# A sixth Strassen group, early branch weights, early bias sums and tanh gates in an encoder layer on one core

## The chip, the cores and the metric

The kernel runs on one core of a Trainium2 chip. Its engines are TensorE (PE in the profile; its weight loads are PEld), VectorE (DVE), ScalarE (ACT), GpSimd (POOL) and SyncE (SP), which here only issues DMA transfers. The metric is device time in microseconds (us). The kernel before took 1932.01 us (median of three runs, 1930.99 to 1932.27).

## What is computed

One encoder layer on 1024 tokens of width 1024, all in fp32:

```python
h = x + 0.5 * swiglu(rms_norm(x, n1), wg1, wu1, wd1)      # FFN 1, hidden width 2816
u = rms_norm(h, nm)
z = u @ w_in                                              # 1024 x 4352: qA kA vA qB kB vB gA gB
yA = neighbourhood_attention_2d(qA, kA, vA, rpb)          # 8 heads of 64, learned bias, band mask
yB = windowed_gqa_sink(rope(qB), rope(kB), vB, sink)      # 8 query heads, 2 key heads, window 128
merged = sigmoid(gA) * (yA @ w_branch_a) + sigmoid(gB) * (yB @ w_branch_b)
h = h + merged @ w_out
h = h + 0.5 * swiglu(rms_norm(h, n2), wg2, wu2, wd2)      # FFN 2
return rms_norm(h, nf)
```

## The kernel before

Every large fp32 product is made of three products of numbers with shortened mantissa: each operand is split into a high part (a cast on ACT, line 93) and a low part (a subtraction, line 94, on DVE or on POOL), and `mm3` (lines 142 to 150) multiplies high by high, high by low and low by high. So each block costs matmuls on PE, one cast on ACT and one "lo split" on DVE or POOL.

The stages follow one another in time as they do in the reference. FFN 1's gate and up products (0 to about 430 us) and most of the input projection (640 to 840 us) are made by Strassen's method in `products`: a group of two pairs of column blocks takes seven smaller products for each half, 14 products of 12 matmuls, 128 x 512 each. The input projection has 34 column blocks: five groups (20 blocks) go through `products`, and 14 gate blocks are left. These are made by `gate` as plain products of 48 matmuls each, and serve as filler between the small steps of attention. The down products of the FFNs and the product with `w_out` are Strassen products too, in the class `Down`: a list of entries (77 for FFN 1: seven products P2, P1, P5, P6, P3, P7, P4 by 11 blocks), each of which is prepared by `prep` (operands summed on DVE or POOL, two hi and two lo splits) up to seven entries ahead of PE and then multiplied in 12 matmuls. `loads` holds further calls by entry; `evict` (line 602) adds finished sums to the result.

Attention (840 to 1122 us) runs over 64 units, 32 of windowed attention and 32 of neighbourhood attention, in a pipeline of three: `scores` of one unit, `turn` (transposes, softmax's values split) of the one before, `values` of the one before that, and `filling` between them, which draws steps of six matmuls from `filler`: the gate blocks, then branch B (`branch_b`, the eight column blocks of yB @ w_branch_b times its gate), then the first two blocks of branch A. For each of the eight heads of neighbourhood attention `load_bias` (line 1089) adds the bias to two masks on DVE, in the middle of attention. What `filler` has left at the end of attention is drained at once; the rest of branch A and the preparation of the product with `w_out` come next.

The program text is written in the order of the work, and a scheduler then gives each engine its own list of instructions, in which each engine works strictly in order; a few are pinned to their place. SP and POOL issue DMA transfers, also in order. Buffers come from rings by tag: `raw` (four), `ws` (eight), `xs` (two), `hs` (six), and PSUM banks by tags `g` and `d`, four each.

Of the kernel before, what the change touches and what calls it, by code (L numbers as in the profile page):

```python
# [36 lines left out]
def trunk_kernel(ctx, tc, x, xt, n1, wg1, wu1, wd1, nm, win, rpb, sink, wa, wb, wo,  # L37
# [54 lines left out]
    def split(dst_hi, dst_lo, src, eng=None):  # L92
        nc.scalar.copy(dst_hi, src)  # L93
        (eng or nc.vector).tensor_tensor(dst_lo, src, f32v(dst_hi), op=ALU.subtract)  # L94
# [139 lines left out]
    def products(src, n, after, at_end, extra, ring, by_hand=False, last=PRODUCTS):  # L234
# [34 lines left out]
        def load_ahead(i):  # L269

            for m in range(2):
                ahead[i, m] = main.tile([P, 1024], F32, tag="ws", bufs=8, name=nm_("ahead"))
                fetch(ahead[i, m], i, m, 0)
# [14 lines left out]
        def pieces(q):  # L288

            i, p, m = seq[q]  # L290
            if i and (i, p, m) in early:
                a = ahead[i, m][:, 512 if p == "P2" else 0:][:, :512]
# [95 lines left out]
    def behind(prods):  # L388

        run, load_ahead = prods[2:4]  # L390

        def post(t):
            if t >= 3:
                drain(run, 10)
            if t in (3, 4):
                load_ahead(t - 2)

        return post
# [278 lines left out]

    def behind_ffn1(n):
        down.at_end(n)
        if n <= 60 and spread:  # L680
            nc.sync.dma_start(*spread.pop(0))

# [194 lines left out]
    groups = [[(12, 13), (14, 15)], [(16, 17), (0, 1)], [(4, 5), (8, 9)], [(2, 3), (6, 7)], [(10, 11), (18, 19)]]  # L877
# [62 lines left out]

    pin = tc.keep_in_program_order
# [65 lines left out]

    def keep_u():

        h, l = rhs(T4)  # L1010
        for i in range(2):
            r = raw4()
            nc.sync.dma_start(r.rearrange("p (t f) -> p t f", t=2), u_d[2 * i:2 * i + 2].rearrange("t p f -> p t f"))
            cols = slice(i * 256, i * 256 + 256)
            v = [a[:, :, cols].rearrange("p c (t x) -> p c t x", t=2) for a in (h, l)]
            split(v[0], v[1], r.rearrange("p (t c x) -> p c t x", t=2, c=4))
# [41 lines left out]
    hook(2, gate_first)  # L1058
    hook(1, keep_u)
    pg = products(lambda i, m, half: w_cols(win[0], groups[i][m][half] * P), NG, store_z, at_end, (2, 3), range(8, 16),  # L1060
                  last=("P1", "P2", "P5", "P6", "P7", "P4", "P3"))
    down.into(transition(down1, gain, to_strassen, behind(pg), 2), pg)
# [4 lines left out]
    mask_a = masks[:, :768].rearrange("p (s k) -> p s k", s=2)  # L1067
    mask_b = masks[:, 768:]
    nc.sync.dma_start(mask_a, c_mask_a.rearrange("s p k -> p s k"))
# [12 lines left out]
    def bias_slot(s):  # L1082
        return fa[:, 768 * s:768 * s + 768].rearrange("p (e k) -> p e k", e=2)

    def load_bias(s, h):
        braw = raw4()[:, :384]
        nc.sync.dma_start(braw, bias_d[h])
        for e in range(2):
            nc.vector.tensor_tensor(bias_slot(s)[:, e, :].rearrange("p (d r w) -> p d r w", d=3, r=ROWS),
                                    braw.rearrange("p (r d w) -> p d r w", d=3, w=8),  # L1090
                                    mask_a[:, e, :].rearrange("p (d r w) -> p d r w", d=3, r=ROWS), op=ALU.add)

    def prep_a(hp):
# [18 lines left out]
        yield  # L1112
        yield
        yield
# [31 lines left out]
    def fetch_branch(r, w, dc):  # L1146
        nc.sync.dma_start(r.rearrange("p (c f) -> p c f", f=P), w_cols(w, dc * P))
        return r

    def branch_w(w, dc, eng=None, r=None):  # L1150

        t = ws4()
        if r is None:
            r = fetch_branch(raw4()[:, :512], w, dc)
        split(t[:, :512], t[:, 512:], r, eng)
        return [t[:, k:k + 512].rearrange("p (c f) -> p c f", f=P) for k in (0, 512)]

# [13 lines left out]
    def split_y(slots, r0, eng):  # L1171
# [6 lines left out]
        split(h, l, r, eng)  # L1178

    a_order = [dc for p in range(4) for dc in (p, p + 4)]  # L1180
    a_mm, a_raw = [], {}
# [391 lines left out]
```

## Time and profile before

| | us |
|---|---|
| median of three runs | 1932.01 |
| profiled execution | 1931.21 |
| its span | 1929.4 |
| PE busy | 1919.3 |
| DVE busy | 1434.0 |
| ACT busy | 944.2 |
| POOL busy | 296.1 |

The granted clock was 0.999 in this execution. A row of the timeline has the start, the duration, the engine, the line, the operation, and "output<-inputs" by the program's names with the tile sizes; in square brackets stands the idle time before it and what ended it. A row of the waits has engine, line and tile, what it waited for, the total, the number of times and the longest. A row of a table of windows has the window, then its length, then PE, PEld, DVE, ACT and POOL busy (number of instructions), the granted clock, the share of the DMA engines and GB/s. A matmul's duration is pipelined: the next one starts before it ends. PE is busy in 99% of the span.

### The profile page before, as it was taken

To read this page: it belongs to the slowest core of one execution; us is meant where nothing else is said; L and a number is where in the kernel's file an instruction comes from. 1 tells how busy PE (TensorE), PEld (TensorE's weight loads), DVE (VectorE), ACT (ScalarE), POOL (GpSimd) and SP (SyncE) were. 2 spreads that over 40 slices of the span, in tenths; PEclk is the share of its full clock that TensorE was granted. 3 is DMA by queue.
4 is the path that set the end of the run, shared out by engine and by line. 5 is a ranking of instruction groups with operands and counts; after the bars stand their busy time and mean duration, and the time that the engine had idled before them with its cause. 6 is when DMAs were issued, how large, how long until landed. Compare 5 with 4: busy or idle time off the path is not lost.

```text
span 1929.4 us, 25478 instructions
## 1 busy us (share of the span) xinstructions
PE 1919.3 (99%) x8956; PEld 1602.7 (83%) x8956; DVE 1434.0 (74%) x2560; ACT 944.2 (49%) x1826; POOL 296.1 (15%) x432
## 2 busy tenths in 40 slices
PE   9999999999999999999999999999999999999998
PEld 8888888888888888888888888888888888888886
DVE  8987765668957778678888856889676566569864
ACT  7532333344446543477777862365333333344453
POOL 0011100013300112211122231010111001005210
PEclk9999999999999999999999999999999999999999
DMA  6244323285334467753459676443422322493341
GB/s 267 95 167 166 138 100 125 87 298 215 92 106 138 158 202 240 218 166 102 116 130 195 188 240 212 170 153 121 147 98 103 127 87 106 145 340 114 115 142 61
DMA packets 151745, 298.70 MB, mean 155 GB/s; under 512 B 14912, under 2 KB 64448, under 8 KB 151616
## 3 DMA queue, kind: packets, MB, share of 16 engines
q1 hardware_dynamic: 123072, 210.53, 33.3%
q0 software_dynamic: 27824, 85.48, 13.3%
q8 instruction: 71, 1.16, 0.2%
q10 hardware_dynamic: 720, 1.05, 0.1%
q14 instruction: 58, 0.48, 0.1%
HBM read 210.50 MB, written 88.27 MB: 155 GB/s over the span
## 4 chain that ended last, share of the span: by engine, by line
PE 96%; DVE 2%; ACT 1%; DMA 0%; issue 0%; POOLq 0%; POOL 0%; DVEq 0%
PE g L145 18%; PE g L147 18%; PE g L149 18%; PE d L149 12%; PE d L145 12%; PE d L147 12%; PE d L1315 2%; PE g L1329 1%; PE d L1294 1%; PE d L1295 1%; PE g L1334 1%; PE d L138 1%; DVE ar L94 0%; DMA ahead<-in_w_in_dram 0%; DMA n1c<-in_ffn_norm_dram 0%
## 5 line engine op out<-in xcount | busy, mean ns | idle before, releaser
L145 PE MATMUL g<-ar,ws 128*128 128x512 f32 x1128 | 422.6, 395 | 0.3 <-DVE fa L602 0.3
L147 PE MATMUL g<-ar,ws 128*128 128x512 f32 x1128 | 416.7, 390 | 0.0
L149 PE MATMUL g<-ar,ws 128*128 128x512 f32 x1128 | 416.3, 390 | 0.0
L145 PE MATMUL d<-ar,ws 128*128 128x512 f32 x736 | 281.9, 390 | 0.5 <-ACT ws L309 0.5
L147 PE MATMUL d<-ar,ws 128*128 128x512 f32 x736 | 281.4, 389 | 0.1
L149 PE MATMUL d<-ar,ws 128*128 128x512 f32 x736 | 281.2, 389 | 0.1
L149 PEld LDWEIGHTS g<-ar,ws 128*128 128x128 f32 x1128 | 211.7, 188 | 44.8
L147 PEld LDWEIGHTS g<-ar,ws 128*128 128x128 f32 x1128 | 211.8, 188 | 44.6
L145 PEld LDWEIGHTS g<-ar,ws 128*128 128x128 f32 x1128 | 206.4, 188 | 36.4 <-issue 0.7
L312 DVE TENSOR_TENSOR ws<-raw,ws 128x512 fp32r<-128x512 f32 x204 | 139.3, 689 | 98.9 <-ACT ws L309 97.9
L309 ACT CAST ws<-raw 128x512 fp32r<-128x512 f32 x204 | 125.0, 620 | 142.2 <-PE g L149 63.8
L145 PEld LDWEIGHTS d<-ar,ws 128*128 128x128 f32 x736 | 138.1, 188 | 29.4 <-ACT ws L309 0.9
L147 PEld LDWEIGHTS d<-ar,ws 128*128 128x128 f32 x736 | 138.1, 188 | 29.3 <-DVE ar L814 0.5
L149 PEld LDWEIGHTS d<-ar,ws 128*128 128x128 f32 x736 | 138.1, 188 | 29.1 <-DVE ws L312 0.5
L93 ACT CAST ws<-raw 128x512 fp32r<-128x512 f32 (+1 forms) x121 | 81.0, 669 | 144.7 <-PE d L149 66.7
L94 DVE TENSOR_TENSOR ws<-raw,ws 128x512 fp32r<-128x512 f32 (+1 forms) x119 | 94.0, 792 | 60.7 <-ACT ws L93 60.5
L415 POOL DMA_DIRECT2D hid<-fx x91 | 49.3, 542 | 432.3 <-DVE fx L475 288.6
L93 ACT CAST ar<-raw 128x512 fp32r<-128x512 f32 (+1 forms) x83 | 56.0, 679 | 93.7 <-PE g L147 55.0
L94 DVE TENSOR_TENSOR ws<-ar,ws 128x512 fp32r<-128x512 f32 x114 | 98.2, 866 | 4.0 <-ACT ws L93 3.9
L145 PE MATMUL g<-ws,ws 128*128 128x512 f32 x232 | 90.9, 392 | 0.0
L149 PE MATMUL g<-ws,ws 128*128 128x512 f32 x232 | 90.4, 390 | 0.0
L147 PE MATMUL g<-ws,ws 128*128 128x512 f32 x232 | 90.3, 389 | 0.0
(313 smaller groups left out, 3604.8 us busy)
## 6 DMA issues: line engine op xcount, KB each, us to landing
raw<-hid SPq DMA_DIRECT2D x70, 512.0 KB
hid<-fx POOLq DMA_DIRECT2D x91, 256.0 KB, 2.3
ar<-in_ffn_w_down_dram SPq DMA_DIRECT2D x32, 512.0 KB
raw<-in_ffn_w_up_dram SPq DMA_DIRECT2D x31, 512.0 KB
raw<-in_ffn_w_gate_dram SPq DMA_DIRECT2D x27, 512.0 KB
raw<-in_w_in_dram SPq DMA_DIRECT2D x27, 512.0 KB
hid<-fa POOLq DMA_DIRECT2D x51, 256.0 KB, 2.6
ar<-zs_d POOLq DMA_DIRECT2D x48, 256.0 KB, 5.0
```

The costliest lines, as they stand in the source:

```text
L93: nc.scalar.copy(dst_hi, src)
L94: (eng or nc.vector).tensor_tensor(dst_lo, src, f32v(dst_hi), op=ALU.subtract)
L138: nc.tensor.transpose(pt[:, c * P:(c + 1) * P], xs[:, (half * 4 + c) * P:(half * 4 + c + 1) * P], ident)
L145: nc.tensor.matmul(b, lhs[0], r[0], start=first, stop=False, **kw)
L147: nc.tensor.matmul(b, lhs[0], r[1], start=False, stop=False, **kw)
L149: nc.tensor.matmul(b, lhs[1], r[0], start=False, stop=last, **kw)
L309: nc.scalar.copy(w[0][:, :512], a)
L312: nc.vector.tensor_tensor(w[0][:, 512:], a, f32v(w[0][:, :512]), op=ALU.subtract)
L415: nc.gpsimd.dma_start(hid[PRODUCTS.index(p), i], src)
L1294: nc.tensor.matmul(b[:, :nw], un["q"][s], un["kd"][s][:, k0 * P:k1 * P], start=True, stop=False)
L1295: nc.tensor.matmul(b[:, :nw], un["q"][s], un["kl"][s][:, k0 * P:k1 * P], start=False, stop=True)
L1315: nc.tensor.transpose(pt[:, i * P:(i + 1) * P], un["pr"][s][:, i * P:(i + 1) * P], ident)
```

## The change

Five things are changed together.

- The blocks 20 to 23 (four gate blocks) become a sixth Strassen group of the input projection, so `gates` has 10 entries instead of 14. The ring of its operand tiles, the early loads of the first two groups (`early_rooms`, `sooner`) and the fetch of `u` (`fetch_u`) are adapted.
- The 16 blocks of the branch weights are split on ACT and DVE behind FFN 1's products (`wab_fetch`, `wab_split`, `wab_put`), one block in every four products, and kept in DRAM (`wab_d`) in split form. In the branches `fetch_w` loads them on POOL's queue.
- The sums of bias and mask (two for each of eight heads) are made behind the entries of the first down product (`bias_fetch`, `bias_add`, `bias_put`: a fetch at entry 2 + 6h, the adds at 5 + 6h, the write at 10 + 6h) and kept in DRAM (`bm_d`). In attention `fetch_bias` loads them.
- The gates use tanh: sigmoid(g) = (1 + tanh(g/2))/2, with (tanh + 1) times the product in one instruction and the factor 1/2 put into the product with `w_out` (0.5 for 1.0).
- The y splits move from POOL to DVE, filling follows a new table of shares (`n_b` = 46 units at 40/46 twice, then 0.8, then 1.5), and the value sums of two heads are made by one instruction where there were two.

The core of the diff:

```diff
-    groups = [[(12, 13), (14, 15)], [(16, 17), (0, 1)], [(4, 5), (8, 9)], [(2, 3), (6, 7)], [(10, 11), (18, 19)]]
+    groups = [[(12, 13), (14, 15)], [(16, 17), (0, 1)], [(4, 5), (8, 9)], [(2, 3), (6, 7)], [(10, 11), (18, 19)],
+              [(20, 21), (22, 23)]]
...
+    def bias_add(h):
+        for e in range(2):
+            o = biased[0][4 + e]
+            pin(nc.vector.tensor_tensor(o.rearrange("p (d r w) -> p d r w", d=3, r=ROWS),
+                                        biased[0][2 + h % 2].rearrange("p (r d w) -> p d r w", d=3, w=8),
+                                        biased[0][e].rearrange("p (d r w) -> p d r w", d=3, r=ROWS), op=ALU.add))
...
+    for h in range(8):
+        for e, f in ((2, bias_fetch), (5, bias_add), (10, bias_put)):
+            k = e + 6 * h
+            down.loads.setdefault(k, []).insert(0, lambda d, f=f, h=h: f(h))
...
+    def wab_split(i):
+        r, h, l = cast[i], hs(F32R), hs(F32R)
+        pin(nc.scalar.copy(h, r))
+        pin(nc.vector.tensor_tensor(l, r, f32v(h), op=ALU.subtract))
+        cast[i] = h, l
+
+    def wab_put(i):
+        for k, a in enumerate(cast.pop(i)):
+            nc.gpsimd.dma_start(wab_d[i, :, k * 512:k * 512 + 512], a)
...
     def behind_ffn1(n):
         down.at_end(n)
         if n <= 60 and spread:
             nc.sync.dma_start(*spread.pop(0))
+        for e, f in ((4, wab_put), (2, wab_split), (0, wab_fetch)):
+            i, k = divmod(80 - e - n, 4)
+            if k == 0 and 0 <= i < 2 * NC8:
+                f(i)
...
+    def fetch_w(i):
+        t = ws4()
+        nc.gpsimd.dma_start(t, wab_d[i])
+        mix["w", i] = [t[:, k:k + 512].rearrange("p (c f) -> p c f", f=P) for k in (0, 512)]
+
+    def open_gate(dc):
+        r = mix["rb", dc]
+        pin(nc.scalar.activation(r, r, AF.Tanh, scale=0.5))
...
             for n in range(2):
                 sl = slice(n * 512, (n + 1) * 512)
-                nc.vector.tensor_tensor(merged(dc)[:, sl], bs[n], rb[:, sl], op=ALU.mult)
+                nc.vector.scalar_tensor_tensor(out=merged(dc)[:, sl], in0=rb[:, sl], scalar=1.0, in1=bs[n],
+                                               op0=ALU.add, op1=ALU.mult)
...
-    rate = (nfill - 44) / 64.0
-    spent = 3.0
-
-    def filling(share):
+    n_b = 46
+    spent = 0.0
+
+    def filling(n):
         nonlocal spent
-        spent += rate * share
+        spent += len(gates) * 4 / n_b if n < n_b else 0.8 if n < 60 else 1.5
         drain(fill, int(spent))
         spent -= int(spent)
...
-    down = Down(4, wo[0], 1.0, place, quarter, {k: left_d[i] for i, k in enumerate(("P5", "P6", "P3", "P7"))},
+    down = Down(4, wo[0], 0.5, place, quarter, {k: left_d[i] for i, k in enumerate(("P5", "P6", "P3", "P7"))},
```

How the lists of the engines change is seen at two places. The lines of the new code are some ten further on: the split is line 98 (94 before), the sums of `prep` are L572 and L574 (L561 and L563 before), and L705 is the add of bias and mask. DVE in the first down product, kernel before; `raw` holds the hidden values, `ar` the weights, and each pair of L94 rows is the lo splits of one entry:

```order
529 L561 TENSOR_TENSOR ar_3100<-ar_3479,ar_3100 128x512
530 L94 TENSOR_TENSOR ws_3623<-raw_3501,ws_3623 128x512
531 L94 TENSOR_TENSOR ws_3624<-ar_3100,ws_3624 128x512
532 L561 TENSOR_TENSOR ar_3100<-ar_3479,ar_3100 128x512
533 L94 TENSOR_TENSOR ws_3644<-raw_3549,ws_3644 128x512
534 L94 TENSOR_TENSOR ws_3645<-ar_3095,ws_3645 128x512
535 L563 TENSOR_TENSOR ar_3095<-ar_3100,ar_3095 128x512
```

The same entries in the changed kernel, where the two adds of one head stand ahead of the splits of entry 23:

```order
552 L572 TENSOR_TENSOR ar_3230<-ar_3621,ar_3230 128x512
553 L98 TENSOR_TENSOR ws_3793<-raw_3695,ws_3793 128x512
554 L98 TENSOR_TENSOR ws_3794<-ar_3225,ws_3794 128x512
555 L705 TENSOR_TENSOR hs_3495<-hs_3493,hs_3491 128x384
556 L705 TENSOR_TENSOR hs_3496<-hs_3493,hs_3492 128x384
557 L574 TENSOR_TENSOR ar_3225<-ar_3230,ar_3225 128x512
558 L98 TENSOR_TENSOR ws_3814<-raw_3695,ws_3814 128x512
559 L98 TENSOR_TENSOR ws_3815<-ar_3225,ws_3815 128x512
```

Such a pair stands in this list eight times, six entries apart, and nothing else moved between these rows.

DVE at the end of branch B, kernel before. `ar_10187` is the product of gate and branch, `ar_10554` and `ar_10679` hold `w_out`, and the last value product has long been written:

```order
1654 L1213 TENSOR_TENSOR ar_10187<-g_10448,xs_10443 128x512
1655 L1213 TENSOR_TENSOR ar_10187<-g_10449,xs_10443 128x512
1656 L94 TENSOR_TENSOR ar_10717<-ar_10554,ar_10717 128x512 x2
1657 L561 TENSOR_TENSOR ar_10554<-ar_10679,ar_10554 128x512
1658 L1437 TENSOR_TENSOR raw_10540<-g_10481,raw_10540 128x512
1659 L1437 TENSOR_TENSOR raw_10540<-g_10482,raw_10540 128x512
```

The changed kernel at the same place. `g_10554`, `g_10601` and `g_10620` are the value products of the last three units, L1348 and L1351 write them to `fa`, and `ar_10642` and `ar_10757` hold `w_out`:

```order
1664 L1281 SCALAR_TENSOR_TENSOR ar_9531<-xs_10381,g_10450 128x512
1665 L1348 TENSOR_TENSOR s_771_6976<-g_10554,s_771_6976 64x256
1666 L1351 TENSOR_TENSOR fa<-g_10554,s_771_6976 64x128 x2
1667 L98 TENSOR_TENSOR ws_10571<-d_10573,ws_10571 128x2x128
1668 L98 TENSOR_TENSOR ws_10572<-d_10578,ws_10572 128x2x128
1669 L98 TENSOR_TENSOR ar_10792<-ar_10642,ar_10792 128x512
1670 L1348 TENSOR_TENSOR s_771_6976<-g_10601,s_771_6976 64x256
1671 L572 TENSOR_TENSOR ar_10642<-ar_10757,ar_10642 128x512
1672 L1351 TENSOR_TENSOR fa<-g_10601,s_771_6976 64x128 x2
1673 L575 TENSOR_TENSOR ar_10757<-ar_10757 128x512
1674 L1348 TENSOR_TENSOR s_771_6976<-g_10620,s_771_6976 64x256
```

The split of a `w_out` block (row 1669) now stands ahead of the writes of the last two units. On SP the eight loads of `w_out` go out as three of `ar_10757`, two of `ar_10642`, a gate block, two of `ar_10642` (the first of these is the one that row 1669 needs) and one of `ar_10757`; before, that block was the fifth.

More of the change, by code (lines that the diff above doesn't have):

```diff
@@ L1260, in units_a @@
             qs, kd, kl, va = heads_a[hp]
-            for s in range(2):
-                load_bias(s, 2 * hp + s)
             for j in range(NTT):
@@ L1379, in trunk_kernel @@
     drain(fill)
-    t = new_ar(2, F32)
-    for i in range(2, NC8):
-        a_raw[i] = fetch_branch(t[:, (i - 2) // 2, i % 2 * 512:i % 2 * 512 + 512], wa[0], a_order[i])
-    split(slot(22), slot(23), fa[:, 3072:4096])
+    for i in range(4, 6):
+        fetch_w(NC8 + i)
     for t in range(4):
```

218 lines of the change are left out of this document (129 added, 89 removed).

## The prediction

> **What bounds the kernel now.** I read the engine table of the page first, then the waits of PE, then its timeline.
>
> ```profile
> PE 1919.3 (99%) x8956; PEld 1602.7 (83%) x8956; DVE 1434.0 (74%) x2560; ACT 944.2 (49%) x1826; POOL 296.1 (15%) x432
> PE g L733 <- POOL ident masks.py:199: 1.5, 1, 1.5
> PE d L145 <- ACT ws L309: 0.5, 1, 0.5
> PE d L1315 <- DVE ws L94: 0.3, 1, 0.3
> PE g L145 <- DVE fa L602: 0.3, 1, 0.3
> 99.62 0.39 PE L147 MATMUL g<-ar,ws 128*128 128x512 f32 x1
> ...
> 100.98 0.39 PE L147 MATMUL g<-ar,ws 128*128 128x512 f32 x1
> 994.47 0.71 PE g L1329 x6
> ```
>
> PE waits 2.6 us in the whole span, so TensorE issue is the bound nearly everywhere and a matmul taken out should show in full. Its price is the step between starts, not the 0.39 us shown: six steps from 99.62 to 100.98 are 1.36 us, 0.227 us each. The 256-column value matmuls take 0.71/6 = 0.12 us. Every other engine matters only where it becomes late. So the question is where the moved work stands beside an engine that is already full, and the windows answer that (columns: PE, PEld, DVE, ACT, POOL busy):
>
> ```profile
> 300.00:420.00 120.00, 120.00 (x531) 99.41 (x530) 71.41 (x109) 44.91 (x78) 11.40 (x21) 1.00 0.42 148
> 460.00:520.00 60.00, 60.00 (x266) 49.70 (x265) 59.59 (x66) 25.54 (x45) 29.68 (x18) 1.00 0.27 84
> 700.00:800.00 100.00, 100.00 (x443) 82.81 (x442) 80.84 (x116) 39.13 (x67) 22.13 (x41) 1.00 0.76 235
> 1020.00:1080.00 60.00, 60.00 (x364) 53.13 (x363) 52.69 (x163) 49.05 (x125) 10.36 (x19) 1.00 0.76 171
> 1180.00:1240.00 60.00, 60.00 (x267) 49.67 (x266) 57.97 (x89) 21.43 (x35) 8.70 (x16) 1.00 0.57 202
> ```
>
> DVE is full in two places: the first down product (59.59 of 60) and the start of the wo product (57.97 of 60). In FFN 1 it has 49 us free of 120, in the input projection 19 of 100, in attention 7 of 60.
>
> **The Strassen group (L939 to L943 of the new code).** Four plain gate blocks of 48 matmuls go, 192; one group of 14 products of 12 comes, 168. That is 24 matmuls of 512 columns fewer, 24 x 0.227 = **-5.4 us**. The group's side work runs where DVE uses 80.84 of 100, and 14 products are 38 us with about 31 us of DVE work beside them; cost nothing, covered by those 19 us in 100. It also takes 44 us of filler from attention, which branch B and the first of branch A now fill.
>
> **Branch weights behind FFN 1.** Sixteen casts on ACT and sixteen lo splits on DVE, of the shape of these rows:
>
> ```profile
> L312 DVE TENSOR_TENSOR ws<-raw,ws 128x512 fp32r<-128x512 f32 x204 | 139.3, 689 | 98.9 <-ACT ws L309 97.9
> L309 ACT CAST ws<-raw 128x512 fp32r<-128x512 f32 x204 | 125.0, 620 | 142.2 <-PE g L149 63.8
> ```
>
> That is 0.62 and 0.69 us, one pair in each 10.9 us of PE (four products). FFN 1 has DVE free for 4.4 us in each such stretch. Taken as nothing; its cover would be gone only if DVE were past 94% there. The 32 writes on POOL's queue stand behind `hid` writes that nothing waits for soon, the 16 loads on SP ahead of weights that are fetched eight products early. Both ends: 0 and one missed pair, 0.7 us.
>
> **Bias and mask sums behind the down product.** Eight pairs of adds leave attention and enter the first down product.
>
> ```profile
> L1089 DVE TENSOR_TENSOR fa<-raw,masks 128x384 f32<-128x384 f32 x16 | 8.5, 549 | 0.1
> 936.90 1.02 DVE L1089 TENSOR_TENSOR fa<-raw,masks 128x384 f32<-128x384 f32 x2
> 482.85 0.69 DVE L563 TENSOR_TENSOR ar<-ar,ar 128x512 f32<-128x512 f32 x1
> 483.45 0.68 DVE L94 TENSOR_TENSOR ws<-raw,ws 128x512 fp32r<-128x512 f32 x1
> 484.06 1.78 DVE L94 TENSOR_TENSOR ws<-ar,ws 128x512 fp32r<-128x512 f32 x1
> 485.88 0.69 DVE L563 TENSOR_TENSOR ar<-ar,ar 128x512 f32<-128x512 f32 x1
> 483.68 1.61 POOL L566 TENSOR_TENSOR ar<-ar,ar 128x512 f32<-128x512 f32 x1 [1.42 <-DVE ar L563]
> 516.47 1.78 DVE L94 TENSOR_TENSOR ar<-ar,ar 128x512 fp32r<-128x512 f32 x1
> 518.17 0.68 DVE L94 TENSOR_TENSOR ar<-raw,ar 128x512 fp32r<-128x512 f32 x1
> 519.64 0.39 PE L145 MATMUL g<-ar 128*128 128x512 f32 x1
> ```
>
> In the full stretch one entry costs DVE 485.88 - 482.85 = 3.03 us, while PE needs 12 x 0.227 = 2.72, so the lead of the splits shrinks by 0.3 us an entry. The smallest lead is at entry 33: its lo split ends at 516.47 + 1.78 = 518.25, PE starts on it at 519.64, a lead of 1.4 us. After that POOL is out of the way and the lead grows again. The new order puts the pairs before entries 11, 17, 23, 29, 35 and so on; those before 17, 23 and 29 lie in the full stretch. A pair is 1.02 us of busy time and, back to back, about 0.94 us of DVE (an add is 0.47 from start to start: the pair of 1.02 less one 0.55), so three are 2.8 us. Less the 1.4 us of lead: **+1.4 us** of PE standing. Ends: 0, if DVE's slow splits absorb the adds, and 4.7 us, if each pair costs one more stretched split as at 484.06 (three times 1.78 - 0.68 = 1.1 on top). I take 1.4: in the order each pair stands between a lo split and L574 (L563 before), the instruction that releases POOL, so POOL is idle while they run. Their loads and writes on SP (a fetch three entries before the add, the write five behind it) wait for adds that DVE has already passed; what is queued there is the next weights, with five entries of slack. DVE gains the 8.5 us in attention.
>
> The stretched split beside POOL's L566 (1.78 against 0.68 us; it ends 0.55 us after POOL does) is what the Trainium skill, "SBUF — State Buffer", section "Who interferes with whom", describes: a DVE instruction with two inputs in SBUF contends with a GpSimd instruction that reads SBUF, and the one that issues first keeps the shared pair for its whole length. The trace agrees; by that rule an add that met L566 would pay up to 1.61 us, which is the third case below.
>
> **Attention.** DVE loses the adds and 32 small sums and takes over six y splits of 128x1024 from POOL; the sigmoid's table load goes. Whole-stage sums hardly move. Locally, four y splits at 1.22 us (the row of L1438 below shows that shape) stand within some 17 us in which DVE has 17 x 7.31/60 = 2.1 us free, plus 1.1 us from adds that left: 4.9 - 3.2 = 1.7 us over. Ends 0 and 1.7; the pipeline of three units absorbs part of it, and PE has stood only 0.3 us for DVE here: **+0.5 us**.
>
> **End of attention and wo.** Before, the last value product was long done when branch B ended. Now the last three units stand between branch B and branch A, and on DVE their writes stand behind a split that needs a block of `w_out`.
>
> ```profile
> 1163.74 6.16 SPq L538 DMA_DIRECT2D ar<-in_w_out_dram  x8
> 1166.31 1.29 DVE L1213 TENSOR_TENSOR ar<-g,xs 128x512 f32<-128x512 f32 x2 [4.15 <-PE g L149]
> 1174.34 1.14 ACT L93 CAST ar<-ar 128x512 fp32r<-128x512 f32 x2 [7.25 <-DMA ar<-in_w_out_dram]
> 1174.99 1.30 DVE L94 TENSOR_TENSOR ar<-ar,ar 128x512 fp32r<-128x512 f32 x2 [7.39 <-ACT ar L93]
> 1178.60 1.22 DVE L1438 TENSOR_TENSOR ar<-ar,raw 128x1024 f32<-128x1024 f32 x1
> 1209.76 1.29 DVE L1437 TENSOR_TENSOR raw<-d,raw 128x512 f32<-128x512 f32 x2 [1.49 <-PE d L149]
> ```
>
> DVE already waited 7.39 us there, at no cost, as PE had branch A to do. The block was the fifth transfer and landed 1174.34 - 1163.74 = 10.6 us after the first issue (2.1 us each). In the new order it is the seventh: 10.6 us if the rate is set by latency, 14.8 if by bytes. Its slot comes free about 3.4 us before branch B's end (12 matmuls and 6 small ones), so it lands 7.2 to 11.4 us after that end. Behind it on DVE, 1.5 us of work frees the bank of unit 63; PE wants it after 42 matmuls of 512 and 18 small ones, 42 x 0.227 + 18 x 0.12 = 11.6 us. So 8.7 to 12.9 against 11.6, and by the same sum the bank of unit 64 (2.1 us on) at 10.8 to 15.0 against 12.5: 0 to 2.5 us of standing. I take **+0.8 us**, nearer the low end, since all eight issues took 6.16 us and so the transfers run beside one another. DVE's remaining 32 us then end close to the start of the wo product as before (1.49 us of idle at 1209.76 is the slack).
>
> **Sum.** -5.4 + 1.4 + 0.5 + 0.8 = -2.7 us. The profiled execution took 1931.2 us (span 1929.4), 0.8 below the median of 1932.0. From the median the change comes out at 1929.3; I say 1929.2.
>
> **Rivals.**
> 1. The cover holds everywhere: only the 5.4 us count, 1926.6; if the 0.3 us standing of L1315 and the like go as well, 1925.5. For it: 2.6 us of waits in all. Against it: a lead of 1.4 us cannot hide 2.8.
> 2. The adds meet POOL's L566: 4.7 us instead of 1.4, -5.4 + 4.7 + 0.5 + 0.8 = +0.6, 1932.6. For it: 1.78 against 0.68 us. Against it: their place ahead of the instruction that releases POOL. By the skill's rule on the shared port this would be the outcome only if POOL were already running.
> 3. Slower: the w_out block at the end of attention. The branch weights are now POOL's loads of 0.5 MB on the same DMA engines; if five of these go ahead of it, it is the twelfth transfer, 12 x 2.1 - 3.4 = 22 us after branch B's end, and PE, which can bear about 10.1, stands 11.9 us: -5.4 + 1.4 + 0.5 + 11.9 = +8.4, 1940.4. It turns the sign for a measurement (+3.9) once the block lands 17.6 us after branch B. For it: ACT's 7.25 us of waiting. Against it: the weights are asked for several products earlier.
>
> **Chances.** Likeliest (adds cost their lack of lead, the rest little) 0.47, own range 1927.5 to 1931.5; rival 1 0.25; rival 2 0.13; rival 3 0.15. Within 0.2% of 1932.0 (3.9 us, about what a measurement of this kernel tells from no change) is 1928.1 to 1935.9. Faster: rival 1 and a third of the likeliest, 0.41; same: the rest of the likeliest and rival 2, 0.44; slower: rival 3, 0.15. The range takes in rival 1 and half of rival 3: 1925.0 to 1936.5.
>
> **What would show it.** PE's matmul groups down by 24 in all. PE standing 1 to 2 us at about 520 us for an `ar` split of DVE, then none until about 650. In attention the waits of L1315 and the value products under 2 us together. DVE's w_out split some 8 to 11 us after branch B's last product, and PE waiting for DVE under 2.5 us there. I am wrong if PE stands more than 3 us in any of these places, if the lead in the projection's first products is gone because of the larger number of blocks to fetch, or if a stall appears in FFN 1, where I costed the 16 splits at nothing.

## The result and the profile after

The changed kernel takes 1937.08 us (median of seven runs, 1936.09 to 1937.83), the kernel before 1931.92 (seven runs, 1930.99 to 1932.27): a ratio of 1.0029, with a 95% interval of 1.0020 to 1.0038. It is slower by 5.2 us, where 1929.2 was forecast. The profiled execution has a span of 1935.9 us, 6.5 more than before.

The page of the changed kernel, its engine table and the two groups in which matmuls went and came:

```profile
PE 1919.7 (99%) x8932; PEld 1601.4 (83%) x8932; DVE 1450.7 (75%) x2535; ACT 944.7 (49%) x1836; POOL 303.5 (16%) x470
...
L149 PE MATMUL g<-ar,ws 128*128 128x512 f32 x1096 | 416.0, 395 | 2.6 <-ACT raw L1290 2.1
...
L149 PE MATMUL d<-ar,ws 128*128 128x512 f32 x760 | 293.9, 393 | 4.2 <-issue 2.1
```

The 24 matmuls are gone: the first group had 1128 before and the second 736, on three lines each, so that 96 went and 72 came (8956 in all before). Yet PE is busy 0.4 us more than before and also waits more. The waits of PE:

```profile
PE g L149 <- ACT raw L1290: 2.1, 1, 2.1
PE d L149 <- issue: 2.1, 1, 2.1
PE d L149 <- ACT ar L95: 1.9, 1, 1.9
PE g L798 <- POOL ident masks.py:199: 1.5, 1, 1.5
PE g L149 <- DVE raw L1517: 0.4, 1, 0.4
```

Only the fourth was there before. For the other time, the windows (PE, PEld, DVE, ACT, POOL busy, granted clock, share of the DMA engines, GB/s):

```profile
300.00:420.00 120.00, 120.00 (x531) 99.38 (x530) 75.98 (x117) 48.76 (x86) 19.99 (x37) 1.00 0.61 204
700.00:800.00 100.00, 100.00 (x443) 82.84 (x442) 74.45 (x105) 37.52 (x65) 21.61 (x39) 1.00 0.76 231
1080.00:1086.00 6.00, 4.09 (x27) 3.43 (x25) 5.76 (x16) 5.72 (x15) 4.73 (x9) 1.00 0.91 296
1086.00:1090.00 4.00, 4.00 (x13) 2.96 (x12) 3.61 (x9) 3.15 (x5) 0.52 (x1) 0.57 1.21 277
1106.00:1109.00 3.00, 2.96 (x9) 2.24 (x9) 1.09 (x3) 1.21 (x2) 0.00 (x0) 0.58 1.22 267
1180.00:1185.00 5.00, 4.56 (x13) 3.31 (x13) 4.92 (x10) 3.15 (x5) 0.00 (x0) 0.66 1.08 406
```

The kernel before, from 1086 us:

```profile
1086.00:1090.00 4.00, 4.00 (x24) 3.43 (x23) 3.26 (x12) 3.58 (x12) 1.69 (x2) 1.00 0.66 253
```

After each of the three waits there is a stretch at a low clock. The three windows with 0.57 to 0.66 hold some time at full clock too; a window cut to the stretch itself shows a clock of 0.50 for 3.41 us each time (from 1086.01, 1106.49 and 1181.58). PE counts as busy there, but issues 13 matmuls where the kernel before issued 24 (1086 to 1090). So PE's waits alone undercount. To add both up, I took for each matmul the time by which its start lies later than the usual step behind the one before (the median step between two matmuls of these sizes in the kernel before; 0.227 us for 512 columns), and summed that by place:

| place, us | before | after | difference |
|---|---|---|---|
| 840 to 940 | 2.9 | 2.4 | -0.5 |
| 940 to 980 (the bias adds stood here) | 2.6 | 1.6 | -1.1 |
| 980 to 1080 | 3.6 | 3.5 | -0.1 |
| 1080 to 1120, branch B with the last units | 1.4 | 9.5 | +8.1 |
| 1120 to 1160, branch B (without units before, with units now) | 0.2 | 1.5 | +1.3 |
| 1160 to 1200, the last units and the first `w_out` blocks | -0.1 | 5.2 | +5.2 |

That is +12.9; less the 5.4 us of the 24 matmuls and 0.8 us of small waits at 654 and 675 us that went, +6.7, close to the 6.5 of the span. The three waits row by row, from the timeline:

```profile
1080.75 1.06 ACT L95 CAST ar<-raw 128x1024 fp32r<-128x1024 f32 x1
...
1083.77 1.03 ACT L95 CAST ar<-raw 128x1024 fp32r<-128x1024 f32 x1
...
1084.85 0.73 PE L149 MATMUL d<-ar,ws 128*128 128x512 f32 x2 [1.91 <-ACT ar L95]
...
1102.71 0.62 ACT L1384 ACTIVATE fa<-fa,nmx 128x384 f32<-128x384 f32 x1
1102.84 0.82 PE L1397 MATMUL d<-ident,fa 128*128 128x128 f32 x6
1103.21 0.69 DVE L1281 SCALAR_TENSOR_TENSOR ar<-xs,g 128x512 f32<-128x512 f32 x1
...
1104.63 1.63 ACT L95 CAST ws<-d 128x384 fp32r<-128x384 f32 x4
...
1105.14 1.95 DVE L98 TENSOR_TENSOR ws<-d,ws 128x384 fp32r<-128x384 f32 x4 [0.26 <-ACT ws L95]
...
1105.80 1.11 PE L149 MATMUL d<-ar,ws 128*128 128x512 f32 x2 [2.14 <-issue]
```

- **First wait**, 2.07 us from the usual start, in branch B's first column. PE wants the second chunk of y. ACT's list has the cast of the third chunk (1080.75) ahead of that of the second (1083.77); ACT is busy 5.72 of 6 us there.
- **Second wait**, 2.38 us, in its third column. PE wants a `d` bank, which holds transposed values of a unit. ACT casts these (1104.63) and DVE splits them (1105.14) only behind the next unit's exponentials and scaling and, on DVE, two gate products. The profile says "issue", and the first of the four splits ends just before PE goes on.

```profile
1160.98 4.79 SPq L549 DMA_DIRECT2D ar<-in_w_out_dram  x5
...
1166.33 1.66 SPq L549 DMA_DIRECT2D ar<-in_w_out_dram  x3
...
1176.93 0.62 ACT L95 CAST ar<-ar 128x512 fp32r<-128x512 f32 x1 [5.54 <-DMA ar<-in_w_out_dram]
...
1177.58 0.37 ACT L1347 COPY s<-g 64x256 f32<-64x256 f32 x1
1177.58 0.69 DVE L98 TENSOR_TENSOR ar<-ar,ar 128x512 fp32r<-128x512 f32 x1 [5.67 <-ACT ar L95]
...
1177.85 2.00 ACT L1290 ACTIVATE raw<-raw 128x1024 f32<-128x1024 f32 x2
1179.13 0.57 DVE L1351 TENSOR_TENSOR fa<-g,s 64x128 f32<-64x128 f32 x2
...
1179.80 0.47 PE L149 MATMUL g<-ar,ws 128*128 128x512 f32 x1 [2.14 <-ACT raw L1290]
...
1181.40 0.66 PE L149 MATMUL g<-ar,ws 128*128 128x512 f32 x1 [0.44 <-DVE raw L1517]
```

- **Third wait**, 2.30 and then 0.60 us. The block of `w_out` was issued at 1166.33 and landed at 1176.9, which is 12.2 us after branch B's last product (1164.7). ACT and DVE both stood behind it. The copy and the sums that free the bank of unit 63 came next. The profile puts the wait down to ACT's two tanh, but in the program the matmul at 1179.80 waits for the copy of unit 63 (L1347, ended by 1177.95) and for its sums on DVE (L1351, ended at 1179.70), not for the tanh. The 0.60 us are a wait for L1517, which stands in DVE's list behind further `w_out` work.

In the first down product nothing stands:

```profile
517.56 1.78 DVE L98 TENSOR_TENSOR ar<-ar,ar 128x512 fp32r<-128x512 f32 x1
...
519.79 0.39 PE L149 MATMUL g<-ar 128*128 128x512 f32 x1
```

The lead at entry 33 is 519.79 - 519.34 = 0.45 us (1.4 before).

### The profile page after: what moved, and what is told of

The parts are those of the page before. It is cut to its first block, busy times and chain, and to the rows that moved or that the text cites. A ratio compares the mean times of both kernels' runs of the same rounds, so it can differ in the third digit from the quotient of the medians.

```text
span 1935.9 us, 25636 instructions
## 1 busy us (share of the span) xinstructions
PE 1919.7 (99%) x8932; PEld 1601.4 (83%) x8932; DVE 1450.7 (75%) x2535; ACT 944.7 (49%) x1836; POOL 303.5 (16%) x470
## 4 chain that ended last, share of the span: by engine, by line
PE 95%; DVE 2%; DMA 1%; ACT 1%; issue 1%; SPq 0%; POOLq 0%; POOL 0%; DVEq 0%; ACTq 0%
PE g L149 17%; PE g L151 17%; PE g L153 17%; PE d L149 12%; PE d L151 12%; PE d L153 12%; PE d L1397 2%; PE g L1416 1%; PE d L1378 1%; PE g L1411 1%; PE d L1379 1%; PE d L142 1%; DMA ar<-in_w_out_dram 1%; DVE ar L98 0%; DMA raw<-zr_d 0%
## 5 line engine op out<-in xcount | busy, mean ns | idle before, releaser
L149 PE MATMUL g<-ar,ws 128*128 128x512 f32 x1096 | 416.0, 395 | 2.6 <-ACT raw L1290 2.1
L151 PE MATMUL g<-ar,ws 128*128 128x512 f32 x1096 | 411.2, 391 | 0.0
L153 PE MATMUL g<-ar,ws 128*128 128x512 f32 x1096 | 409.9, 390 | 0.0
L149 PE MATMUL d<-ar,ws 128*128 128x512 f32 x760 | 293.9, 393 | 4.2 <-issue 2.1
L151 PE MATMUL d<-ar,ws 128*128 128x512 f32 x760 | 292.9, 391 | 0.2 <-DVE ar L879 0.2
L153 PE MATMUL d<-ar,ws 128*128 128x512 f32 x760 | 292.9, 391 | 0.0
L153 PEld LDWEIGHTS g<-ar,ws 128*128 128x128 f32 x1096 | 206.0, 188 | 43.5
L151 PEld LDWEIGHTS g<-ar,ws 128*128 128x128 f32 x1096 | 206.0, 188 | 42.8
L149 PEld LDWEIGHTS g<-ar,ws 128*128 128x128 f32 x1096 | 201.6, 188 | 39.7 <-ACT raw L1290 2.5
L322 DVE TENSOR_TENSOR ws<-raw,ws 128x512 fp32r<-128x512 f32 x210 | 143.5, 689 | 90.2 <-ACT ws L319 89.3
L149 PEld LDWEIGHTS d<-ar,ws 128*128 128x128 f32 x760 | 142.5, 188 | 34.1 <-issue 2.7
L153 PEld LDWEIGHTS d<-ar,ws 128*128 128x128 f32 x760 | 143.2, 188 | 30.1 <-DVE ws L322 0.5
L151 PEld LDWEIGHTS d<-ar,ws 128*128 128x128 f32 x760 | 143.2, 189 | 30.0 <-DVE ar L879 0.6
L95 ACT CAST ws<-raw 128x512 fp32r<-128x512 f32 (+1 forms) x107 | 70.6, 660 | 132.8 <-PE d L153 67.5
L98 DVE TENSOR_TENSOR ws<-raw,ws 128x512 fp32r<-128x512 f32 (+1 forms) x107 | 84.7, 792 | 49.7 <-ACT ws L95 49.5
L98 DVE TENSOR_TENSOR ws<-ar,ws 128x512 fp32r<-128x512 f32 x114 | 93.9, 828 | 11.3 <-ACT ws L95 11.3
L1384 ACT ACTIVATE fa<-fa,nmx 128x385 f32<-128x385 f32 (+3 forms) x128 | 75.4, 590 | 36.6 <-DVE nmx L1381 35.7
L149 PE MATMUL g<-ws,ws 128*128 128x512 f32 x232 | 90.9, 392 | 0.0
L153 PE MATMUL g<-ws,ws 128*128 128x512 f32 x232 | 90.4, 390 | 0.0
```

The costliest lines, as they stand in the source:

```text
L95: hi = nc.scalar.copy(dst_hi, src)
L149: nc.tensor.matmul(b, lhs[0], r[0], start=first, stop=False, **kw)
L151: nc.tensor.matmul(b, lhs[0], r[1], start=False, stop=False, **kw)
L153: nc.tensor.matmul(b, lhs[1], r[0], start=False, stop=last, **kw)
L322: nc.vector.tensor_tensor(w[0][:, 512:], a, f32v(w[0][:, :512]), op=ALU.subtract)
L1384: nc.scalar.activation(pr, pr, AF.Exp, scale=-1.0, bias=nmx[:, s:s + 1], accum_out=ssum[:, s:s + 1])
```

## The experiments

My theory at the start: each of the three waits has its own local cause (the `w_out` block, the order of ACT's list, the pace of the last units), and the Strassen group earns what was forecast. The rivals: the group, which took attention's filler, or the y splits that went to DVE are the cause of all. Times stand beside those of the kernel before on the same chip, 1931.58 to 1931.74 us (medians).

**The third wait alone.** `wo_behind` orders ACT's and DVE's preparation of the product with `w_out` behind the last split of y, and thus behind the last units:

```diff
             while self.done < min(n, len(self.seq)):
-                self.prep(self.done)
+                with ExitStack() as st:
+                    for ins in self.behind:
+                        st.enter_context(tc.issue_after(ins.ins))
+                    self.prep(self.done)
...
+    down.behind = mix["y_last"]
```

> The changed kernel with one edit: the preparation of the w_out product is held behind the last y split on ACT and DVE, so that no cast or lo split of a w_out block stands ahead of the writes of the last two units. Theory A (the third wait, 2.9 us of standing plus 2.2 us at a lower clock behind it, comes from these instructions waiting for their block): about 1932.0, and PE stands less than 0.5 us between 1175 and 1185 us. Rival (DVE is behind there in any case, and the work only comes due at the start of the w_out product): 1935 to 1937, with a new wait of PE near 1210 us.

Measured: 1931.67 us against 1931.65, ratio 1.0000 (0.9991 to 1.0010). Its waits:

```profile
PE d L150 <- issue: 2.1, 1, 2.1
PE d L150 <- ACT ar L95: 1.9, 1, 1.9
```

The third wait is gone (late starts of 0.6 us from 1160 to 1200, 5.2 in the changed kernel), the others are unchanged. So the `w_out` block ahead of the last units is worth 5.4 us in the medians; in the two profiled executions 4.5 us of late starts went at this place, 2.9 of them the wait, the rest the low clock behind it. The remaining two waits and the small delays around them still eat all that the 24 matmuls save. In this execution they were followed by no low clock, so that a part of the difference between the two profiled executions (9.5 against 6.9 us of late starts from 1080 to 1120) isn't this edit's:

```profile
1085.00:1090.00 5.00, 4.45 (x23) 3.65 (x24) 4.71 (x11) 4.70 (x10) 1.66 (x4) 1.00 1.20 283
1105.00:1109.00 4.00, 3.77 (x19) 3.21 (x20) 2.28 (x7) 2.17 (x5) 0.53 (x1) 1.00 1.21 262
```

**The group undone, and the group alone.** `five_groups` takes the sixth group out of the changed kernel; `sixth_only` puts it into the kernel before, with nothing else.

```diff
-              [(20, 21), (22, 23)]]
```

> The changed kernel without the sixth Strassen group: 14 plain gate blocks again, spread over the same 46 units, all else as changed. Theory A (branch B beside the last units, not the group, makes the two waits in attention): the waits near units 46 to 52 and the one at the w_out block stay, PE gets 24 matmuls back, 5.4 us: about 1942.5. Rival (too little filler for each unit): the two waits in attention, 4.5 and 4.4 us over the usual pace, go: 1933 to 1935.

> The kernel before with the sixth Strassen group alone: ten gate blocks spread over the whole attention at 1.16 steps a unit, where there were 1.66; branch B, the bias sums and the gates as before. Theory A: branch B stays behind attention, no wait above 1 us, so most of the 5.4 us shows: 1926.5 to 1928.5. Rival (attention lives on its filler: with less of it for each unit DVE and ACT set the pace): 1932 to 1938, with many waits of L1315 and L1329 of some 0.3 us.

Measured: `five_groups` 1941.5 us (ratio 1.0056, 1.0039 to 1.0072; four runs, 1938.29 to 1943.88), 4.4 more than the changed kernel, so that within the new plan the group is worth about what 24 matmuls cost. Its profiled execution is the fastest of the four:

```profile
1106.84 1.09 PE L1396 MATMUL d<-ident,fa 128*128 128x128 f32 x6 [1.84 <-DVE nmx L1380]
1110.17 0.77 PE L149 MATMUL d<-ar,ws 128*128 128x512 f32 x1 [2.24 <-issue]
```

Two waits of 2.0 and 2.5 us from their usual starts stand in branch B without the group too, so the group isn't needed for them, though they aren't the same two: the one for the second chunk's cast is not there. The third wait shrinks to 0.4 us. So the edit doesn't leave the waits as they were, as my theory had it; it moves them.

`sixth_only` 1938.8 us (1.0039; 1.0024 to 1.0054): alone it makes the kernel before slower by 7.2 us, where my theory had it gain. Its late rows:

```profile
1101.61 0.85 PE L1316 MATMUL d<-ident,fa 128*128 128x128 f32 x6 [0.79 <-DVE fa L1307]
...
1113.64 0.55 PE L1316 MATMUL d<-ident,fa 128*128 128x128 f32 x3 [1.77 <-DVE fa L1307]
...
1121.68 0.55 PE L1316 MATMUL d<-ident,fa 128*128 128x128 f32 x3 [1.08 <-DVE ws L94]
```

These are transposes: the first two wait for softmax's scaling on DVE, the third for a split on DVE. The four gate blocks were cover for attention: with them the kernel before draws 1.66 steps a unit, without them 1.16, and DVE and ACT no longer get a unit done in that time. In the new plan of the changed kernel (branch B and A among the units) the group pays.

**The y splits back on POOL.** `y_pool` has the four places where y is split for branch B and A call POOL again.

```diff
-            split_y(Y_A[min(n - 59, 2)], 512 + min(n - 59, 2) * P, nc.vector)
+            split_y(Y_A[min(n - 59, 2)], 512 + min(n - 59, 2) * P, nc.gpsimd)
```

> The changed kernel with six of the seven y splits' low parts back on POOL; the casts stay on ACT. Theory A (the first wait is for the cast on ACT, the second for the softmax chain between branch B's products): 1936 to 1938, the first wait no shorter. Rival (DVE has too much with the y splits): the first two waits shrink to under 1 us together, 1929 to 1932.

Measured: 1937.94 us (1.0032; 1.0019 to 1.0045), like the changed kernel. The waits that concern it:

```profile
PE d L149 <- issue: 2.5, 1, 2.5
PE d L151 <- POOL ar L98: 1.6, 2, 1.1
PE g L149 <- ACT raw L1290: 3.3, 1, 3.3
```

The first wait is shorter than I expected (1.2 us, now for a split on POOL, where it was 2.07 for the cast), the second stays and the third grows (2.1 in the same list of the changed kernel). Late starts from 1080 to 1120 are 9.0 us against 9.5. So the place of the splits isn't the cause of the loss.

**Order and pace, on top of `wo_behind`.** `y_order` splits the chunks of y in the order of their use, and also splits the second chunk one step earlier in the last gate block; `steady` draws branch B faster and more evenly (1.0 step in each call of `filling` for 0.8; there are two calls a unit); `both` has the two; `late_branch` spreads the gate blocks over 54 units for 46. In `steady` and `both` the third chunk of branch A is multiplied before its last units are written, so that a part of the computation is changed; the work is the same.

```diff
-        split(h, l, r, eng, True)
+        with ExitStack() as st:
+            for ins in mix.get("y_before", ()):
+                st.enter_context(tc.issue_after(ins.ins))
+            mix["y_before"] = split(h, l, r, eng, True)
...
-                                     6: lambda: [split_y(Y_B[1], P, nc.vector), fetch_y(3 * P)]})
+                                     5: lambda: [split_y(Y_B[1], P, nc.vector), fetch_y(3 * P)]})
...
-        spent += len(gates) * 4 / n_b if n < n_b else 0.8 if n < 60 else 1.5
+        spent += len(gates) * 4 / n_b if n < n_b else 1.0 if n < 60 else 1.5
...
-    n_b = 46
+    n_b = 54
```

> wo_behind with the y splits of branch B kept in the order of their use (second chunk ahead of the third; on ACT the third was ahead of the second). Theory A (the first wait is for the second chunk's cast, which stands behind the third's): the wait at about 1085 us falls from 2.1 to under 1 us, the one at 1105 stays at 2 to 2.5: about 1930. Rival (ACT has too much work there, whatever its order): the wait stays above 1.5 us, 1931 to 1932.

> wo_behind with one step of filler in each call (1.0) while branch B runs beside attention, where there were 0.8, so that no unit goes without. Theory A (the second wait comes from a unit with too little filler between its scores and its transposes, so that the split of its transposes, which frees a PSUM bank, is late): the wait at 1105 falls under 1 us, the one at 1085 stays: about 1929.5. Rival (the second wait is set by the order on ACT and DVE, not by the pace of PE): it stays at 2 us or more, 1931 to 1933.

> wo_behind with both edits, the order of the y splits and one step a call. Theory A: neither wait above 1 us, the 5.4 us of the sixth group show nearly in full: 1927 to 1928.5. Rival: 1930 to 1932, the waits move to other units.

> wo_behind with the ten gate blocks spread over 54 units in place of 46, so that branch B meets ten units and not eighteen, with less filler for each unit before (0.74 in a call, where there were 0.87). Theory A (branch B beside the units costs, but so does little filler, as the sixth group alone showed): 1931 to 1935, many waits of L1397 of 0.3 to 1 us and one of 2 us where branch B starts. Rival (only branch B costs): 1928 to 1930.

Measured: `y_order` 1931.94 us (1.0002; 0.9993 to 1.0011), `steady` 1936.21 (1.0024; 1.0013 to 1.0034), `both` 1937.24 (1.0031; 1.0019 to 1.0044), `late_branch` 1933.83 (1.0010; 1.0000 to 1.0019). In `y_order` the first wait is gone (by the order or by the earlier split, which the edit doesn't separate), but two others of 0.9 and 1.0 us come in its place, one for transposed values and one for weights, and the second stays at 2.4. `steady` and `both` are slower than either of my theories had them: PE no longer waits for the bank at 1105 us, and waits for the branch weights instead (`both`):

```profile
PE g L150 <- DMA ws<-wab_d: 7.0, 2, 6.3
```

`late_branch` shortens the waits in branch B to under 1 us and leaves more to drain at the end, where PE then waits 2.6 us for DVE at the start of the product with `w_out`. So the first two waits are not one mistake of order: each edit uncovers what was late next.

**The second wait.** `cast_first` adds to `y_order` that, from unit 44 on, the next unit's bias sums and exponentials stand behind the casts and splits of the transposed values. `w_early` then asks for the second block of branch weights in the last gate block.

```diff
+                for ins in pipe[1]["split"] if npair[0] >= 44 else ():
+                    st.enter_context(tc.issue_after(ins.ins))
                 nc.vector.tensor_tensor_reduce(out=pr[:, ext:], in0=b[:, :nw], in1=un["bias"][s][:, moff:moff + nw], scale=-1.0,
...
-        fetch_w(1)
...
-                                     1: lambda: [fetch_w(0), fetch_gate(0)],
+                                     1: lambda: [fetch_w(0), fetch_gate(0), fetch_w(1)],
```

> y_order with one more order fixed while branch B runs: the bias sums and exponentials of a unit stand behind the two transposed casts and lo splits that were traced ahead of them, on ACT and DVE. Theory A (the wait of 2.4 us at 1105 us is PE waiting for a PSUM bank whose transposes ACT casts only after the next unit's exponentials): the wait falls under 1 us, and with y_order's other small waits the time is 1928.5 to 1930. Rival (branch B's own products need the DMA or DVE at that point): still 2 us at the same product, 1931 to 1932.

> cast_first with the second block of branch weights loaded one gate block earlier, ahead of the loads for the last heads, which share the DMA engines with it. Theory A (the wait of 0.9 us for the weights at 1088 us in y_order is this load): it goes, 0.9 us less than cast_first. Rival (the earlier load takes a buffer of the transposed weights' ring, and the units wait for it): no faster than cast_first.

Measured: `cast_first` 1931.19 us (0.9998; 0.9988 to 1.0007), `w_early` 1932.96 (1.0006; 0.9996 to 1.0016). The wait in `cast_first`, and the window ahead of it:

```profile
1103.44 0.98 PE L1408 MATMUL d<-ident,fa 128*128 128x128 f32 x6 [2.04 <-DVE ws L98]
```

```profile
1095.00:1105.00 10.00, 7.96 (x47) 6.43 (x46) 9.79 (x32) 7.84 (x21) 2.46 (x5) 0.98 1.24 262
```

The kernel before in the same window, and two rows of `cast_first`:

```profile
1095.00:1105.00 10.00, 10.00 (x61) 8.69 (x60) 8.41 (x25) 8.57 (x20) 2.41 (x1) 1.00 0.67 226
1101.22 0.68 DVE L1289 SCALAR_TENSOR_TENSOR ar<-xs,g 128x512 f32<-128x512 f32 x1
...
1102.14 0.68 DVE L1289 SCALAR_TENSOR_TENSOR ar<-xs,g 128x512 f32<-128x512 f32 x1
```

The splits now stand ahead of the next unit's bias sums, and a wait as long stands at a neighbouring product: DVE is busy 9.79 of 10 us. The pace of the units isn't new (1.6 steps a unit against 1.66; from 1087.4 to 1097.0 us the kernel before got three units through DVE, by the starts of softmax's reciprocal). New are branch B's gate products (L1289) beside them, three in these ten us, 0.68 us each. With them DVE is full ahead of the wait. That is the rival of the order theory; but the products at 1101.22 and 1102.14 still stand ahead of the splits that PE wants (1102.74), so this run alone doesn't rule order out. Of the two waits that `y_order` brought, the one for weights is gone in both runs; `w_early` is no faster for its earlier load, as its rival had it.

**The price of the adds.** `adds_twice` makes each pair of the adds of bias and mask twice.

```diff
-        for e in range(2):
+        for e in (0, 1, 0, 1):
```

> The changed kernel with each sum of bias and mask made twice, at the same place (the result is the same). My prediction charged three pairs at 0.94 us against a lead of 1.4 us and so 1.4 us of waiting, while the changed kernel shows none, with a lead of 0.5 us at entry 33. Theory A (the price of a pair was right, and the lead is what absorbs it): three pairs more, 2.8 us, on a lead of 0.5: PE stands about 2.3 us near 519 us. Rival (DVE's list has slack there that the sum of busy times does not show): under 0.5 us.

Measured in one run, with a span of 1937.5 us, 1.6 more than the changed kernel:

```profile
522.16 0.50 PE L151 MATMUL g<-ar 128*128 128x512 f32 x1 [1.79 <-DVE ar L98]
```

PE is 1.95 us late by its usual step. Three pairs more in the full stretch, at 0.94 each, are 2.8, less the lead of 0.45: 2.3. That fits the price of a pair, but only within about 1 us, since this place differs from execution to execution. `w_early` is the same program as the changed kernel up to 1000 us, with the adds once, and in its profiled execution PE stands here too:

```profile
PE d L152 <- DVE ar L98: 1.0, 1, 1.0
```

This is at 518.75 us. `wo_behind`, `y_pool` and `paced_w`, the same there as well, are 0.2 us late, most others nothing. So the adds have used up the lead, and whether PE stands for it is chance.

**Pace and weights together.** `paced` is `cast_first` with 1.0 step a call (1.5 from unit 62). `paced_w` asks for the weights sooner as well: the second block in the last gate block, the others one step earlier in each column. `paced_50` is `paced` with 50 units for the gate blocks.

```diff
-        spent += len(gates) * 4 / n_b if n < n_b else 0.8 if n < 60 else 1.5
+        spent += len(gates) * 4 / n_b if n < n_b else 1.0 if n < 62 else 1.5
...
                 if c == 0:
+                    fetch_w(dc + 2)
...
-                elif c == 1:
-                    fetch_w(dc + 2)
```

> cast_first with one step of filler in each call (1.0) up to unit 62 while branch B runs. Pace theory: the wait of 2.2 us at 1103 us falls under 1 us, 1929 to 1930. Load theory: branch B now runs faster than its weights land, waits of 2 to 6 us for the weights take its place, 1933 to 1937.

> paced with the weights of branch B asked for earlier (the second block in the last gate block, the others one step sooner). Load theory: the waits for weights shrink by about 2 us against paced, 1930 to 1934. Pace theory: as paced.

> paced with the gate blocks spread over 50 units, so that branch B starts some 17 us later, behind most of the loads for the last heads. Load theory: no wait for weights above 1 us, neither of the two waits is left, 1927 to 1929.5. Pace theory (units before 50 get 0.8 steps a call in place of 0.87 and wait more): 1930 to 1932.

Measured: `paced` 1937.2 us (1.0030; 1.0019 to 1.0040), `paced_50` 1936.26 (1.0027; 1.0016 to 1.0037), and `paced_w` 1928.03 (median of ten; nine lie between 1927.28 and 1929.43, the tenth took 6454.84 us and isn't explained), ratio 0.998 (0.997 to 0.999): faster than both kernels, and than either theory had it. The wait of `paced`, and its window ahead of it:

```profile
PE g L150 <- DMA ws<-wab_d: 6.6, 1, 6.6
1095.00:1105.00 10.00, 9.79 (x52) 8.22 (x52) 8.19 (x28) 7.10 (x18) 2.94 (x5) 1.00 1.22 275
```

The one wait of `paced_w` above 0.3 us that the kernel before doesn't have:

```profile
PE d L150 <- DVE nmx L1390: 1.5, 1, 1.5
```

In `paced` the bank wait at 1103 is gone and DVE is busy 8.19 of 10 us. It is gone too in `both`, which lacks `cast_first`'s order; before this place it waits only 0.8 us for weights (1087.8), and its long wait comes later (until 1115.01). So DVE's load fits as the cause of that wait, and `cast_first`'s order isn't needed to be rid of it; but the new pace also moves the gate products in DVE's list, and the two effects aren't separated. (`steady` shows less: it waits 2.3 us for weights at 1088, in which DVE can catch up.) The weights of the next column were issued at 1100.27 and landed at 1114.51, 14.2 us. In `paced_w` a block took 12.6 (1104.38 to 1116.99) and nobody waited. Its late starts from 1080 to 1120 come to 4.0 us (9.5 in the changed kernel), with no low clock; one wait of 1.6 us is left, at 1083.6. `paced_50` met neither theory: it waits 2.2 us for weights in branch B and 3.2 us at 1215 us for DVE at the start of the product with `w_out`.

Why weights take so long, from the DMA issues of the changed kernel from 1080 to 1106 us (KB each, median us to landing):

```profile
ar<-zs_d POOLq DMA_DIRECT2D x12, 256.0 KB, 15.2
ws<-wab_d POOLq DMA_DIRECT2D x3, 512.0 KB, 12.2
```

The operands of the last heads are loaded in the same 26 us, and all 16 DMA engines are busy throughout. `paced_w` doesn't shorten this; it asks earlier.

Not tried: pace and early weights without the new orders of `y_order` and `cast_first`. Whether those two are needed for the gain stays open; on their own they bring nothing that can be measured.

## Why the prediction was wrong

The range (1925.0 to 1936.5) missed the time by 0.6 us and the sign was wrong. Term by term:

- **Strassen group, -5.4.** The count is right, and `five_groups` puts its worth in the new plan at 4.4 us. Its side work cost nothing, as said: DVE has 74.45 us of 100 in the projection. The sentence that branch B and branch A "now fill" the 44 us of filler was half the story. PE has its filler again, but the gate blocks had asked little of DVE, and branch B brings products, tanh and transfers of its own (see attention). `sixth_only` shows what the filler was worth in the old plan: 7.2 + 5.4 = 12.6 us of cover.
- **Branch weights behind FFN 1, nothing.** Right: PE is busy 120.00 of 120 us, DVE 75.98. The other end of the same edit was wrong. I wrote that the weights "are asked for several products earlier" and took that for safe. They take 8 to 14 us to land there, and as soon as the pace was right they were the next thing late (6.6 us in `paced`). The split that left attention came back as a transfer in its busiest stretch.
- **Bias and mask sums, +1.4.** Too high for the changed kernel, which has no wait here. DVE came into the stretch with more lead (12.1 us at entry 20, 7.5 before), so that the lead at entry 33 shrank by 0.95 us and not by 2.8. The margin is thin: the forecast wait stands in one variant with the same program there (0.98 us in `w_early`), so that its absence is partly luck. No add met POOL's sums, as I had argued against rival 2: the eight adds from 440 to 520 us took 0.54 to 0.55 us each. But their neighbours did: over entries 20 to 33 the lead fell by 11.7 us (6.1 before), of which the two pairs there are 1.9; most of the rest are sums and splits of 1.66 to 1.78 us (at 472 to 482 us, for one) that took 0.69 at their place in the kernel before. In attention, where the adds had stood, late starts fell by 1.1 us (940 to 980), which I had only counted against the y splits.
- **Attention, +0.5.** The step that failed most: +8.1 us from 1080 to 1120 us. I had compared the work of DVE and ACT over 17 us with their free time (1.7 us over at most), and let "the pipeline of three units" absorb it. Three things were not in that sum. It had the y splits, but not branch B's own work beside the units, which before came behind attention: from 1080 to 1120 us six gate products on DVE (3.9 us) and three tanh on ACT (3.1 us). It took the free time from the stretch before (52.69 of 60), while in `cast_first` DVE has 9.79 of 10 us of work ahead of the second wait. And it was a sum of work where the order counts: in a list that is worked in order, the cast of the third chunk (1.06 us) and the units' instructions behind it delay the cast that PE wants, 2.07 us of waiting. 4.45 us are the two waits, and 11 matmuls at the low clock behind them 2.2 more.
- **End of attention, +0.8.** The place and the mechanism were right, and the size was off: 5.2 us. The block landed 12.2 us after branch B's end (I gave 7.2 to 11.4), which is 15.95 us after the first of the issues: near the 14.8 of my end by bytes, where I had leaned to the other. From there to the free bank took 2.9 us (I had 1.5): 0.65 for ACT's cast, which I left out, and 2.1 for four instructions on DVE, one of them a sum of `w_out`. So PE stood 2.30 + 0.60 us, and then ran 8 matmuls at the low clock, 1.6 more. Rival 3 has the same wait with another reason for the late block, five weights ahead of it. `wo_behind` confirms the wait; no run tests that reason, and the time of landing doesn't need it.
- **Left out altogether:** the clock after a wait. Of the 13.3 us that came at 1080 to 1120 and 1160 to 1200, 7.35 are waits; 19 matmuls of 512 columns at the low clock, 0.2 us each, account for 3.8 of the rest. The last 2.1 are small delays that I haven't traced.

## What to carry to other kernels

Work that fills one stage is that stage's cover: before a matmul is saved, ask which engines lived behind it, and count their load, with what the new filler itself asks of them, in the few microseconds where it is highest, not over the stage. An operand prepared earlier and kept in DRAM turns compute into a transfer, whose time to land under the load of that stage must be measured and asked for in advance. On engines that work in order, look for an instruction that waits for a transfer, or is ready early, ahead of one that PE wants.

## What the runs showed of the hardware

**Clock after short waits.** Waits of PE of 1.95 us and more were followed, in some executions, by 3.41 us at a clock of 0.50 (6.83 in `steady`), in which a 512-column matmul started every 0.427 us and not every 0.227 (clock 0.57 in the changed kernel's row from 1086), and in others not: `wo_behind` has the same two waits of 2.07 and 2.39 us and a clock of 1.00 behind them. `five_groups` has two such waits, of 2.0 and 2.5 us, and the low clock once (0.59 from 1110 to 1114), from the end of the second. The shortest wait that was followed by it is the 1.95 us of `adds_twice`; one of 2.75 us in `late_branch` (1211 us) was not. The Trainium skill, "TensorE: Matmul & The Clock Gate", "Part 1: The HAM clock gate (the "warmup" mystery)", has the clock halve after an idle window of about 3.4 us that runs freely. The halved clock, the 3.41 us and the chance element agree with the runs; here waits of 2 us were enough, shorter than that window.

**Landing under load.** In the changed kernel a 256 KB load on POOL's queue took a median of 15.2 us to land from 1080 to 1106 us, and 7.5 over the whole kernel (`ar<-zs_d`, 48 loads); in the kernel before it was 5.0.
